# The second layer's attention weights turned in 32x32 blocks by the vector engine, and multiplied as 32-row matmuls on four row groups

## The chip, the core and the metric

The kernel runs on one core of a Trainium2 chip. The metric is the device time of one execution in microseconds; the median of three runs before the change is 858.31 us (855.99 to 860.19). The core has a matrix engine (TensorE, PE in the profile, its weight loads PEld), a vector engine (DVE), a scalar engine (ACT), a general engine (POOL) and a queue engine that issues most DMAs (SP). Each of them works through its own instructions in a fixed order, and they wait for one another by semaphores.

## The reference

Two layers over 512 latent and 256 context tokens of width 1024. Layer 0 is differential attention, layer 1, which the change is about, is grouped-query attention: 8 query heads of 128 share 2 K/V heads, and the 512 latent queries read all 768 keys. Cut to what matters:

```python
def sweep_attention(q, k, v):            # per block of 128 queries
    s = einsum('bqhgd,bkhd->bhgqk', q, k) * Dh ** -0.5
    p = softmax(s, axis=-1)
    return einsum('bhgqk,bkhd->bqhgd', p, v)

def gqa_mixer(h, hc, w_in, w_out, qk_g, cos, sin):
    q, k, v, z = split(h @ w_in)         # k and v from latent and context tokens
    q = rope(rms_norm(q, qk_g[0])); k = rope(rms_norm(k, qk_g[1]))
    return (sweep_attention(q, k, v) * silu(z)) @ w_out

x = x + gate * rms_norm(gqa_mixer(...), post_g)
```

## The kernel before

Every product of the layers is done as three matmuls of operands that are split into a rounded high part and the remaining low part (`mm3`: high x high, high x low, low x high; L145 to L147). The high part is made by a copy on ACT, the low part by a subtraction on DVE or POOL.

Layer 1 goes in these steps. First K and V are projected for six blocks of 128 tokens. V stays in SBUF as a high and a low part, `vh` and `vl`, tokens on the partitions (L1315, L1316). Then Q is projected in four pairs of heads (`q_proj`, on which a rope on DVE and POOL follows) and the gate path Z in eight heads (`z1_proj`). These two are fill work: generators of single matmuls, listed in `FILL1`, which a planner puts between the steps of attention. Their weights come as 512 KB loads on SP into two buffers (`raw`), are split by ACT (L199) and by POOL or DVE (L200), and are held in a few slots.

Attention is a set of streams of steps with due times, in `flow`. A clock in the planner counts matmul time; the step that is due first is written next, and as long as none is due, fill work is written. The streams are `S_` (scores), `T_` (transposes), `M_` (multiplication with V), `X_` (`q_tr`, which transposes Q of a head) and `Y_` (ten steps that sum the rows of the output gate from 512 KB loads, on DVE). The final order on each engine is then set by a scheduler that has the priorities of these steps.

One score unit is one head and 128 queries: six matmuls of 384 columns into one of two PSUM buffers of two banks (`sc`), the maximum on DVE (L1398), its scaling (L1401), the exponential with its sum on ACT (L1404), the reciprocal on DVE (L1405) and the normalisation on POOL (L207) into an SBUF tile `p`, queries on the partitions. The keys have to be on the partitions for the product with V. So for each head, each half of 256 queries and each pair of 128-key blocks, TensorE transposes four 128x128 blocks into a PSUM bank (L1419), ACT copies the high part out (`ah`, L1422), DVE subtracts the low part (`al`, L1423), and six matmuls with 128 rows and 256 columns add the product to the result of this half (`pv_mm`, L152). There are 48 such chunks: 8 heads, 2 halves, 3 pairs of blocks. ACT moves the result to SBUF (L1436), POOL multiplies it with the gate (L1366). At the end `tail1` splits the gated heads (L1482, L1483), the first quarter of the output projection starts with the heads that are there (`out_head`), and the other columns, the sums of squares, the residual `x1` (in SBUF since layer 0) and the stores follow.

## Time and profile before

| what | value |
|---|---|
| median of three runs | 858.31 us |
| profiled execution, its time | 855.26 us |
| profiled execution, its span | 853.5 us |
| mean granted TensorE clock | 0.985 |
| HBM read and written | 70.56 MB, 2.10 MB |

All durations below are those of the profiled execution; its own time is 1.8 us above its span. A row of a group of instructions reads: line, engine, operation, output and inputs, shapes, count, then the busy time in us and the mean of one in ns, then the engine's idle time before them and what ended it. A row of the timeline reads: start and length in us, engine, line, operation, count, and in brackets the idle time before it. For TensorE the length of a matmul contains the passage through the array, so matmuls overlap in the rows, and the distance between starts tells what one costs.

### The profile page before, as it was taken

The page shows a single profiled execution, that of the slowest core. Times are in us where ns is not written, and L with a number is a line of the kernel's source. Part 1 is how long each engine was busy: PE and PEld are TensorE (multiplying, and loading weights), DVE is VectorE, ACT ScalarE, POOL GpSimd, SP SyncE. Part 2 cuts the span into 40 slices and gives each one's busy share as a digit, 9 for nine tenths or more (in the row PEclk, how much of TensorE's full clock was granted, in tenths as well). Part 3 has the DMA queues.
Part 4 walks back from the last instruction along what each step waited for, and adds up shares of the span by engine and source line. Part 5 has one row for each costly group of instructions (what it writes and reads, how often), then busy time and mean ns, then how long its engine had stood idle before and what let it go on. Part 6 is the DMA issues. An engine that isn't in the chain of part 4 may idle for free. (4 is left out here: it accounts for less than half of the span.)

```text
span 853.5 us, 14255 instructions
## 1 busy us (share of the span) xinstructions
PE 808.6 (95%) x5472; PEld 710.3 (83%) x5472; DVE 498.5 (58%) x897; ACT 455.0 (53%) x1001; POOL 412.4 (48%) x390
## 2 busy tenths in 40 slices
PE   7899998999999999999899999989999989999997
PEld 5578887789786899698798898779999879999986
DVE  4425556763666755674437963477346576665634
ACT  5324456565465544565436953465445556676731
POOL 4333564746356663365631321465578736544201
PEclk8999999999999999999899999999999999999999
DMA  9933210122123241222320106030223232210112
GB/s 302 347 100 124 87 38 26 68 80 78 35 95 128 93 143 63 90 72 87 136 95 29 48 27 220 4 105 26 99 99 100 75 99 76 75 50 26 51 48 99
DMA packets 41540, 77.77 MB, mean 91 GB/s; under 512 B 3584, under 2 KB 18688, under 8 KB 41472
## 3 DMA queue, kind: packets, MB, share of 16 engines
q1 hardware_dynamic: 38048, 71.71, 25.4%
q10 hardware_dynamic: 3424, 5.15, 1.7%
q8 instruction: 43, 0.70, 0.3%
q14 instruction: 25, 0.20, 0.1%
HBM read 70.56 MB, written 2.10 MB: 85 GB/s over the span
## 5 line engine op out<-in xcount | busy, mean ns | idle before, releaser
L145 PE MATMUL bk<-whi,h 128*128 128x256 f32 (+1 forms) x592 | 177.3, 302 | 5.1 <-DVE u L1184 3.6
L146 PE MATMUL bk<-wlo,h 128*128 128x256 f32 (+1 forms) x592 | 176.7, 299 | 0.7 <-DVE wlo L200 0.7
L147 PE MATMUL bk<-whi,h 128*128 128x256 f32 (+1 forms) x592 | 176.1, 300 | 0.7 <-DVE h L1222 0.6
L145 PE MATMUL bk<-h,whi 128*128 128x512 f32 (+2 forms) x416 | 148.0, 356 | 2.5 <-DVE vlo L798 1.3
L146 PE MATMUL bk<-h,whi 128*128 128x512 f32 (+2 forms) x416 | 146.3, 352 | 0.0
L147 PE MATMUL bk<-h,wlo 128*128 128x512 f32 (+2 forms) x416 | 146.0, 352 | 0.0
L200 POOL TENSOR_TENSOR wlo<-raw,whi 128x1024 fp32r<-128x1024 f32 x46 | 114.0, 2483 | 61.6 <-ACT whi L199 61.4
L145 PEld LDWEIGHTS bk<-whi,h 128*128 128x128 f32 x592 | 112.7, 190 | 13.8 <-DVE u L1184 3.2
L207 POOL TENSOR_SCALAR p<-p,sm 128x768 f32<-128x768 f32 (+1 forms) x80 | 70.1, 878 | 105.9 <-DVE sm L872 54.0
L146 PEld LDWEIGHTS bk<-wlo,h 128*128 128x128 f32 x592 | 112.8, 190 | 5.7 <-issue 1.3
L147 PEld LDWEIGHTS bk<-whi,h 128*128 128x128 f32 x592 | 112.5, 191 | 4.8 <-DVE h L1222 1.1
L145 PEld LDWEIGHTS bk<-h,whi 128*128 128x128 f32 x416 | 79.3, 191 | 13.9 <-issue 1.8
L869 ACT ACTIVATE p<-sc,sm 128x768 f32<-128x768 f32 (+1 forms) x68 | 59.6, 878 | 54.0 <-DVE sm L866 49.1
L147 PEld LDWEIGHTS bk<-h,wlo 128*128 128x128 f32 x416 | 79.2, 191 | 10.0 <-issue 2.6
L146 PEld LDWEIGHTS bk<-h,whi 128*128 128x128 f32 x416 | 79.4, 191 | 7.7 <-issue 1.3
L199 ACT CAST whi<-raw 128x1024 fp32r<-128x1024 f32 x64 | 67.2, 1051 | 31.2 <-PE bk L146 11.7
L866 DVE TENSOR_REDUCE sm<-sc 128x1 f32<-128x768 f32 (+1 forms) x68 | 60.6, 917 | 17.6 <-PE sc L861 17.6
L929 ACT CAST ah<-bk 128x512 fp32r<-128x512 f32 x56 | 32.0, 589 | 36.7 <-PE bk L926 21.8
L877 DVE SCALAR_TENSOR_TENSOR p<-p,sm,p 128x768 f32<-128x768 f32 (+1 forms) x34 | 43.3, 1274 | 11.1 <-POOL p L207 8.7
L753 POOL TENSOR_TENSOR qr<-qr,rope 128x512 f32<-128x512 f32 x14 | 23.7, 1690 | 50.8 <-DMA sw<-qr 36.8
L861 PE MATMUL sc<-qk,qk 64*128 64x384 f32 (+1 forms) x396 | 44.7, 353 | 2.2 <-ACT p L900 1.2
L930 DVE TENSOR_TENSOR al<-bk,ah 128x512 fp32r<-128x512 f32 x56 | 37.5, 684 | 13.6 <-ACT ah L929 13.5
(247 smaller groups left out, 1721.1 us busy)
## 6 DMA issues: line engine op xcount, KB each, us to landing
raw<-in_a_w SPq DMA_DIRECT2D x30, 512.0 KB, 3.5
araw<-in_ada_w SPq DMA_DIRECT2D x12, 1024.0 KB, 5.1
raw<-in_b_w SPq DMA_DIRECT2D x20, 512.0 KB, 3.5
ag<-in_ada_w SPq DMA_DIRECT2D x32, 256.0 KB, 6.4
raw<-in_w_out SPq DMA_DIRECT2D x16, 512.0 KB, 3.5
sw<-qr ACTq DMA_DIRECT2D x32, 128.0 KB, 2.9
raw<-in_ada_w SPq DMA_DIRECT2D x8, 512.0 KB, 3.7
xt<-in_x SPq DMA_DIRECT2D x4, 512.0 KB, 5.4
```

The source lines that it names most:

```text
L145: nc.tensor.matmul(o, ahi, bhi, start=start, stop=False)
L146: nc.tensor.matmul(o, ahi, blo, start=False, stop=False)
L147: nc.tensor.matmul(o, alo, bhi, start=False, stop=stop)
L199: nc.scalar.copy(hi, r)
L200: eng.tensor_tensor(lo, r, f32(hi), ALU.subtract)
L207: (nc.vector if eng == "v" else nc.gpsimd).tensor_scalar(dst, src, s_, 1.0, ALU.mult, ALU.mult)
L861: prev = nc.tensor.matmul(sc[m][:, j if nk == T else m, :w], a[r, tok], b[r, c], start=i == 0, stop=i == 2)
L866: nc.vector.tensor_reduce(mx, scv, AX.XY if nk == T else AX.X, ALU.max, negate=True)
L869: nc.scalar.activation(pv_, scv, AF.Exp, bias=mx, accum_out=l[:, m:m + 1])
L877: nc.vector.scalar_tensor_tensor(ps_[0], pt, r, ps_[0], ALU.mult, ALU.add)
L929: nc.scalar.copy(ah, tr)
L930: nc.vector.tensor_tensor(al, tr, f32(ah), ALU.subtract)
```

## The change

The probabilities are no longer transposed by TensorE. `p_turn` turns each 128x768 tile `p` on DVE, in 32x32 blocks: partition 32i + r of the result holds key 32k + r, for all 24 blocks k of 32 keys, of the 32 queries 32i to 32i + 31. So each group of 32 partitions has all keys, but only its own queries. Eight turns (two heads, four blocks of queries) fill one tile `pT`, of which there is one.

`pv1_burst` then multiplies two heads at once. For each of 24 blocks of keys and each of the three high and low terms it issues four matmuls with 32 rows and 256 columns, one for each group of 32 partitions, into four PSUM banks; in bursts 0 to 2 two of the banks are one of the score buffers. There are four bursts (numbered 0 to 3 below) of 288 such matmuls, in place of 288 matmuls with 128 rows. High parts are still made on ACT, low parts by DVE and POOL in turn (`ECL`), in chunks of two blocks of keys, with four buffers for each part. V has to lie on every group of 32 partitions: it is stored to DRAM, high and low parts together (`v_dram`), and loaded four times over for each of the two K/V heads (`v_load4`), 3.1 MB each, the second time after burst 1, into the same tile.

Around this: the streams are now `S_`, `B_` (bursts and `tail1`) and `R_` (turns); a unit's due time goes by `TSU` and a burst's 8.6; the list of fill work is in another order; the gate's steps come at every third unit; the last pair of heads, not only the last half of a head, is gated and split after the last burst (`last_pair`), with `out_head` over six heads, and a part of the next output columns is written ahead (`o_next`). To make room, `x1` is stored to DRAM and loaded again at the end, and layer 1's context columns lie in tiles of their own (`h1c`).

```diff
-FILL1 = (('z', 0), ('q', 2), ('q', 1), ('z', 2), ('z', 1), ('q', 3), ('z', 3), ('z', 4), ('z', 5), ('z', 7), ('z', 6))
+FILL1 = (('q', 1), ('z', 0), ('z', 1), ('z', 2), ('q', 2), ('z', 3), ('z', 4), ('q', 3), ('z', 5), ('z', 6), ('z', 7))
...
-GSTEP = 2
+GSTEP = 3
...
+KB = 24
+ECL = 'vp'
+PB = 5
+TSU = 3.4
+LR = 4.5
+LB = 3.5
...
+    x1 = [bp.tile([P, D], F32, name=f"x1_{t}", bufs=1) for t in range(NQ)]
+    h1c_hi, h1c_lo = [bp.tile([P, KT, C], F32R, tag="h1c", name=nm("h1c"), bufs=2) for _ in range(2)]
+    x1_dram = dram.tile([S, D], F32, name="x1_dram")
+    v_dram = dram.tile([T, 2, 2, P], F32, name="v_dram")
...
+        if m < NQ:
+            nc.sync.dma_start(x1_dram[m * P:(m + 1) * P, :], xd)
...
-                    nc.scalar.copy(vh[:, m, :], o)
-                    nc.vector.tensor_tensor(vl[:, m, :], o, f32(vh[:, m, :]), ALU.subtract)
+                    if m // 2 not in vsp:
+                        vsp[m // 2] = t1p.tile([P, 2, 512], F32R, tag="gp", name=nm("vs"), bufs=4)
+                    vs = vsp[m // 2][:, m % 2].rearrange("p (g h d) -> p g h d", g=2, h=2)
+                    og = o.rearrange("p (g d) -> p g d", g=2)
+                    nc.scalar.copy(vs[:, :, 0], og)
+                    nc.vector.tensor_tensor(vs[:, :, 1], og, f32(vs[:, :, 0]), ALU.subtract)
                     close(o)
+                    nc.sync.dma_start(v_dram[m * P:(m + 1) * P], f32(vs))
...
+        vrep = {}
+
+        def v_load4(g):
+            vrep[g] = t1p.tile([P, KB, 2, P], F32R, tag="vr", name=nm("vr"), bufs=1)
+            for i in range(4):
+                nc.sync.dma_start(
+                    f32(vrep[g][32 * i:32 * i + 32]), v_dram[:, g].rearrange("(k p) h d -> p k h d", p=32))
+
+        v_load4(0)
...
-        def s1_units(h, ms):
...
+        pts, pTs = {}, {}
+
+        def s1_unit(h, m):
+            g = h // 4
+            qa, qb = qT[h]
+            sl = slice(m * P, (m + 1) * P)
+            sc = sc2()
...
+            pts[h, m] = pt
+
+        def p_turn(h, m):
+            b, u = h // 2, h % 2 * NQ + m
+            if u == 0:
+                pTs[b] = t1q.tile([P, KB, 256], F32, tag="pT", name=nm("pT"), bufs=1)
+            nc.vector.transpose(
+                pTs[b][:, :, u * 32:u * 32 + 32], pts.pop((h, m)).rearrange("p (k n) -> p k n", n=32))
+
+        def pv1_burst(b):
+            need = 3 if b < 3 else 4
+            while len(lru) < need:
+                ok_ = piece()
+                assert ok_ or len(lru) >= need
+            g, pT = b // 2, pTs.pop(b)
+            os, prev = [pj(256) for _ in range(4 if b == 3 else 2)], None
+            if b < 3:
                 sc = sc2()
...
+                os += [sc[:, 0, :256], sc[:, 1, :256]]
+            for c in range(KB // 2):
+                ah = t1q.tile([P, 512], F32R, tag="ah", name=nm("ah"), bufs=4)
+                al = t1q.tile([P, 512], F32R, tag="al", name=nm("al"), bufs=4)
+                src = pT[:, 2 * c:2 * c + 2].rearrange("p k n -> p (k n)")
+                nc.scalar.copy(ah, src)
+                VP[ECL[c % 2]].tensor_tensor(al, src, f32(ah), ALU.subtract)
                 for e in range(2):
...
+                    kb = 2 * c + e
+                    for t, (v, a) in enumerate(((0, ah), (1, ah), (0, al))):
+                        for i in (3, 2, 1, 0):
+                            r = slice(32 * i, 32 * i + 32)
+                            with after(prev):
+                                prev = nc.tensor.matmul(
+                                    os[i], vrep[g][r, kb, v, :], a[r, e * 256:e * 256 + 256],
+                                    start=kb == 0 and t == 0, stop=kb == KB - 1 and t == 2)
+            gp = t1p.tile([P, 2, 512], F32, tag="gp", name=nm("gp"), bufs=4)
+            pairs[b] = gp.rearrange("p h (m i n) -> p i h m n", m=NQ, i=4)
+            for j in range(2):
+                gT1[2 * b + j] = gp[:, j, :]
+            for i, o in enumerate(os):
+                ov_ = o.rearrange("p (h m n) -> p h m n", h=2, m=NQ)
+                (nc.scalar.copy if i % 2 else nc.vector.tensor_copy)(pairs[b][:, i], ov_)
+                if i < 2 or b == 3:
                     close(o)
...
+            for h in (2 * b, 2 * b + 1):
+                done1.add(h)
+                gate_mul1(h)
+            if b == 1:
+                v_load4(1)
...
-        def last_half(j):
...
+        def last_pair():
+            for h in (KT - 2, KT - 1):
+                VP[EGL].tensor_tensor(gT1[h], gT1[h], szt1[h], ALU.mult)
+            split_g1((KT - 2, KT - 1))
...
-            split_g1(range(KT - 1))
-            last_half(0)
+            split_g1(range(KT - 2))
             w_o.append(get_wout(1, *OUTC1[0]))
             o_pre.extend(sc_quarter(OUTC1[0][1]))
-            add(out_head(o_pre, ghi, glo, w_o[0], OUTC1[0][1]))
+            add(out_head(o_pre, ghi, glo, w_o[0], OUTC1[0][1], KT - 2))
...
-            for ch in range(2):
...
+            for m in range(NQ):
+                n = len(S_)
+                st_ = Step(lambda h=h, m=m: s1_unit(h, m), 1.05, [(qtr[h], 2.5)], at=at_ + TSU * n + 8.6 * ((n + 5) // 8 - 1 if n > 3 else 0))
+                if n >= 2:
+                    st_.lag.append((S_[-2], SLAG1))
+                if n >= PB:
+                    st_.lag.append((R_[n - PB], 0.0))
+                S_.append(st_)
+                R_.append(Step(lambda h=h, m=m: p_turn(h, m), 0.0, [(st_, LR)]))
+                if B_:
+                    R_[-1].lag.append((B_[-1], 0.0))
+            if h == KT - 1:
+                B_.append(Step(tail1, 0.0, [(S_[-1], 0.0)]))
+            if j:
+                B_.append(Step(lambda p=p: pv1_burst(p), 8.6, [(R_[-1], LB)]))
...
-        flow(1, [S_, T_, M_, X_, Y_])
+        flow(1, [S_, B_, R_, X_, Y_])
         drain()
         w_o = w_o[0]
+        last_pair()
+        x1_ = t1q.tile([P, KB, 256], F32, tag="pT", name=nm("x1"), bufs=1)
+        x1 = [x1_[:, 4 * m:4 * m + 4].rearrange("p k n -> p (k n)") for m in range(NQ)]
+        for m in range(NQ):
+            nc.sync.dma_start(x1[m], x1_dram[m * P:(m + 1) * P, :])
+        c, n = OUTC1[1]
+        o_next, w_next = pj(n), {k: ws.get(k) for k in wout_keys(1, c, n) if ws.has(k)}
+        kn = 1024 // n * len(w_next)
+        run(out_proj(o_next, ghi, glo, list(w_next.values()), 0, n, 0, kn))
...
+                elif qi == 1 and m == 0:
+                    o = o_next
+                    run(out_proj(o, ghi, glo, w, m, n, kn))
```

Three places in the programs, by their order on an engine.

On PE in the middle of layer 1's attention, before: `sc` are score buffers, `bk` banks, `kh`, `kl`, `qh`, `ql` the parts of K and Q, `p` the probabilities, `vh` and `vl` V.

```order
L147 MATMUL sc_73<-kh,ql_7956 128x384
L152 MATMUL bk_70<-ah_7983,vh 128x256 x2
L152 MATMUL bk_70<-ah_7983,vl 128x256 x2
L1419 MATMUL bk_71<-ident,p_7810 128x128
L1419 MATMUL bk_71<-ident,p_7864 128x128
L1419 MATMUL bk_71<-ident,p_7810 128x128
L1419 MATMUL bk_71<-ident,p_7864 128x128
L152 MATMUL bk_70<-al_7984,vh 128x256 x2
L152 MATMUL bk_70<-ah_8009,vh 128x256 x2
```

On PE at the start of burst 0, now: the end of the unit ahead of it (two units, 12 matmuls, stand between the last unit that the burst needs and the burst), the first matmuls of the burst, and then projection; `whi`, `wlo` and `h` are a Q projection, `vr` the copied V.

```order
L152 MATMUL sc_74<-kh,qh_6869 128x384
L153 MATMUL sc_74<-kl,qh_6869 128x384
L154 MATMUL sc_74<-kh,ql_6870 128x384
L1466 MATMUL sc_75<-ah_7086,vr_6347 128x256 x2
L1466 MATMUL bk_71<-ah_7086,vr_6347 128x256
L1466 MATMUL bk_72<-ah_7086,vr_6347 128x256
L1466 MATMUL sc_75<-ah_7086,vr_6347 128x256 x2
L1466 MATMUL bk_71<-ah_7086,vr_6347 128x256
L1466 MATMUL bk_72<-ah_7086,vr_6347 128x256
L152 MATMUL bk_70<-whi_6735,h_689_5197 128x256
L153 MATMUL bk_70<-wlo_6736,h_689_5197 128x256
L154 MATMUL bk_70<-whi_6735,h_690_5198 128x256
```

The transposes (L1419) between the multiplications are gone, and a burst stands in one piece, without other matmuls in it; only burst 0 has 14 projection matmuls after its eighth, of which the first three are shown. Bursts 1 and 2 stand behind projection matmuls, 2.9 and 5.6 us of them at the distances of the profile.

On PE at the last score units, before (`h` and `whi` are a Z projection, as fill work):

```order
L147 MATMUL bk_68<-h_689_5199,wlo_7913 128x512
L145 MATMUL sc_72<-kh,qh_8159 128x384
L146 MATMUL sc_72<-kl,qh_8159 128x384
L147 MATMUL sc_72<-kh,ql_8160 128x384
L145 MATMUL sc_72<-kh,qh_8159 128x384
L146 MATMUL sc_72<-kl,qh_8159 128x384
L152 MATMUL bk_71<-ah_8340,vh 128x256 x2
L152 MATMUL bk_71<-ah_8340,vl 128x256 x2
L1419 MATMUL bk_69<-ident,p_8263 128x128
L1419 MATMUL bk_69<-ident,p_8308 128x128
```

On PE behind burst 2, now (`ac` and `ones_r` are the column sum of the gate):

```order
L1466 MATMUL bk_72<-al_8828,vr_8140 128x256
L152 MATMUL sc_74<-kh,qh_8400 128x384
L153 MATMUL sc_74<-kl,qh_8400 128x384
L154 MATMUL sc_74<-kh,ql_8401 128x384
L152 MATMUL sc_74<-kh,qh_8400 128x384
L153 MATMUL sc_74<-kl,qh_8400 128x384
L154 MATMUL sc_74<-kh,ql_8401 128x384
L374 MATMUL bk_72<-ac_8950,ones_r 128x512
L152 MATMUL sc_75<-kh,qh_8400 128x384
L153 MATMUL sc_75<-kl,qh_8400 128x384
L154 MATMUL sc_75<-kh,ql_8401 128x384
```

Six units, one behind the other, stand behind burst 2 with nothing but that column sum between them; the fill work has been used up before, and the first quarter of the output projection comes after the sixth.

On DVE in burst 2, now (`h` are the split heads, L1519 the low part of them, L207 a weight's low part, L1459 a low part of the attention, L1429 and L1433 the small steps of a unit):

```order
L1459 TENSOR_TENSOR al_8520<-pT_8160,ah_8519 128x512
L1429 TENSOR_TENSOR sm_8499<-sm_8497,qrs_8240 128x1
L1459 TENSOR_TENSOR al_8576<-pT_8160,ah_8575 128x512
L1433 RECIPROCAL sm_8454<-sm_8454 128x1
L1433 RECIPROCAL sm_8502<-sm_8502 128x1
L1519 TENSOR_TENSOR h_1276_9031<-gp_7422,h_1275_9030 128x512 x2
L1519 TENSOR_TENSOR h_1276_9031<-gp_8133,h_1275_9030 128x512 x2
L207 TENSOR_TENSOR wlo_8971<-raw_8968,whi_8970 128x1024
L1459 TENSOR_TENSOR al_8632<-pT_8160,ah_8631 128x512
L1459 TENSOR_TENSOR al_8688<-pT_8160,ah_8687 128x512
L1459 TENSOR_TENSOR al_8744<-pT_8160,ah_8743 128x512
L1459 TENSOR_TENSOR al_8800<-pT_8160,ah_8799 128x512
```

On DVE at the end of the attention before, the splits stand in the same way between low parts:

```order
L1423 TENSOR_TENSOR al_8535<-bk_68,ah_8534 128x512
L200 TENSOR_TENSOR wlo_8587<-raw_8584,whi_8586 128x1024
L1483 TENSOR_TENSOR h_1288_8601<-g_974_6952,h_1287_8600 128x512
L1483 TENSOR_TENSOR h_1288_8601<-g_1029_7222,h_1287_8600 128x512
L1483 TENSOR_TENSOR h_1288_8601<-g_1069_7440,h_1287_8600 128x512
L1483 TENSOR_TENSOR h_1288_8601<-g_1121_7706,h_1287_8600 128x512
L1483 TENSOR_TENSOR h_1288_8601<-g_1176_7977,h_1287_8600 128x512
L1483 TENSOR_TENSOR h_1288_8601<-g_1212_8181,h_1287_8600 128x512
L1423 TENSOR_TENSOR al_8555<-bk_69,ah_8554 128x512
L1423 TENSOR_TENSOR al_8624<-bk_68,ah_8623 128x512
```

In both, splits and a weight's low part stand between two low parts of the attention; what has moved is that four splits now come between the low parts of burst 2, where six heads were split at once before. Behind these rows DVE has two turns (L1441) of the last pair and the evictions of the burst (L1475).

144 lines of the change are left out of this document (49 added, 95 removed).

## The prediction

> **What bounds the kernel now.** I read the page's first part, then the busy time by stretches, then PE's waits in the stage that is changed.
>
> ```profile
> span 853.5 us, 14255 instructions
> PE 808.6 (95%) x5472; PEld 710.3 (83%) x5472; DVE 498.5 (58%) x897; ACT 455.0 (53%) x1001; POOL 412.4 (48%) x390
> ```
>
> ```profile
> 675.00:695.00 20.00, 18.53 (x114) 15.66 (x113) 14.92 (x26) 10.36 (x21) 8.89 (x9) 1.00 0.40 118
> 695.00:715.00 20.00, 17.73 (x132) 17.02 (x132) 13.77 (x23) 12.25 (x24) 10.48 (x9) 1.00 0.34 106
> 612.00:848.00 236.00, 231.05 (x1568) 214.64 (x1566) 140.03 (x282) 132.34 (x296) 116.79 (x125) 1.00 0.22 72
> ```
>
> After the stretch come its length and the busy times of PE, PEld, DVE, ACT and POOL, then the granted clock, the DMA share and GB/s. Layer 1's Q and Z projections, attention and output lie between 612 and 848 us. PE is idle there for 236.00 - 231.05 = 4.95 us, most of it in two 20 us stretches, while DVE works 59% of the time, ACT 56% and POOL 49%. So TensorE's order is the clock of this stage: a matmul that leaves it is worth its time, and a wait that is put into it costs its time.
>
> ```profile
> PE bk L1355 <- DVE al L1423: 2.3, 1, 2.3
> PE bk L1355 <- DVE ql L1359: 0.7, 1, 0.7
> ```
>
> These are PE's longest waits after 613 us (total, times, longest): it is DVE, late in its own queue, that holds PE.
>
> **The change part by part.** *Transposes on PE go.* A matmul's own time is longer than its share of the pipeline, so I take distances between starts.
>
> ```profile
> 805.38 0.28 PE L146 MATMUL sc<-wlo,h 128*128 128x256 f32 x1
> 805.50 0.60 PE L1419 MATMUL bk<-ident,p 128*128 128x128 f32 x4
> 805.86 0.48 PE L152 MATMUL bk<-al,vh 128*128 128x256 f32 x2
> 806.18 0.28 PE L147 MATMUL sc<-whi,h 128*128 128x256 f32 x1
> L1419 PE MATMUL bk<-ident,p 128*128 128x128 f32 x192 | 29.0, 274 | 0.2 <-ACT g L1436 0.2
> ```
>
> A 256-column matmul moves the next one by 0.12 us (805.38 to 805.50). Four transposes and two such matmuls take 806.18 - 805.50 = 0.68 us, so four transposes cost 0.68 - 0.24 = 0.44. There are 192/4 = 48 such sets: **-21.1 us**.
>
> *The multiplication itself.* Before, 16 chunks of 3 x 6 = 288 matmuls of 256 columns, 288 x 0.12 = 34.6 us. Now 4 bursts of 24 x 3 = 72 groups, and each group is four 32-row matmuls of 256 columns on four row groups. If the four run side by side, this is again 288 x 0.12. No 32-row matmul is in the trace, but layer 0's scores are pairs of 64-row ones:
>
> ```profile
> 122.02 0.75 PE L890 MATMUL sc<-qk,qk 64*128 64x256 f32 x10
> 382.07 1.00 PEld L861 LDWEIGHTS sc<-qk,qk 64*128 64x128 f32 x12 [0.17 <-issue]
> ```
>
> Five pairs of 256 columns, of which the last matmul takes 0.28: (0.75 - 0.28)/4 = 0.1175 us a pair, what a single full matmul takes. Two row groups run fully side by side, and their weight loads do too: twelve loads in 1.00 us are 0.083 each. I take 0.1175 for four as well: **0**. The bounds are this and 2 x 0.1175 = 0.235, where only two run at once; 0.1175 is the nearer row, since nothing in the pairs shows a limit.
>
> *Change of row groups.* Going into 32-row work and out of it is seen once in the trace for 64 rows:
>
> ```profile
> 381.54 0.60 PE L926 MATMUL bk<-ident,p 128*128 128x128 f32 x4
> 382.07 1.32 PE L861 MATMUL sc<-qk,qk 64*128 64x384 f32 x12
> 383.32 0.38 PE L152 MATMUL bk<-al,vhi 128*128 128x256 f32 x1
> 383.54 0.35 PE L147 MATMUL bk<-h,wlo 128*128 128x384 f32 x1
> ...
> 634.24 0.34 PE L145 MATMUL sc<-kh,qh 128*128 128x384 f32 x1
> 634.42 0.33 PE L146 MATMUL sc<-kl,qh 128*128 128x384 f32 x1
> 634.59 0.34 PE L145 MATMUL sc<-kh,qh 128*128 128x384 f32 x1
> ```
>
> 384 columns take 0.175 (634.24 to 634.59 for two). The transposes should let the pairs start at 381.98, and they start at 382.07; six pairs should take 1.05 and take 1.25; the next matmul takes 0.22 for 0.12. Together 0.09 + 0.20 + 0.10 = 0.4 us. There are five entries (the first burst is split in two by 14 projection matmuls): **+2.0 us**.
>
> *New waits of PE.* The durations:
>
> ```profile
> L1398 DVE TENSOR_REDUCE sm<-sc 128x1 f32<-128x768 f32 x32 | 30.4, 949 | 4.7 <-PE sc L147 4.6
> L1401 DVE TENSOR_TENSOR sm<-sm,qrs 128x1 f32<-128x1 f32 x32 | 7.0, 218 | 0.2
> L1405 DVE RECIPROCAL sm<-sm 128x1 f32<-128x1 f32 x32 | 5.1, 158 | 14.3 <-ACT p L1404 14.1
> L1423 DVE TENSOR_TENSOR al<-bk,ah 128x512 fp32r<-128x512 f32 x48 | 32.3, 685 | 22.3 <-ACT ah L1422 22.3
> L200 DVE TENSOR_TENSOR wlo<-raw,whi 128x1024 fp32r<-128x1024 f32 x8 | 9.8, 1227 | 4.6 <-ACT whi L199 4.4
> L1404 ACT ACTIVATE p<-sc,sm,qrs 128x768 f32<-128x768 f32 x32 | 31.9, 998 | 20.2 <-DVE sm L1401 13.4 <-PE bk L1419 4.3 <-DVE qrs L1340 2.3
> L1404 ACT ACTIVATION_READ_ACCUMULATOR p<-sc,sm,qrs 128x1 f32 x32 | 6.4, 200 | 0.0
> L1422 ACT CAST ah<-bk 128x512 fp32r<-128x512 f32 x48 | 27.3, 589 | 15.7 <-PE bk L1419 14.4 <-PE bk L152 0.7
> L207 POOL TENSOR_SCALAR p<-p,sm 128x768 f32<-128x768 f32 x64 | 62.6, 978 | 88.8 <-DVE sm L872 44.6 <-DVE sm L1405 36.5 <-DVE sm L1401 3.9
> L366 POOL TENSOR_TENSOR ac<-gate,ac 128x512 fp32r<-128x512 f32 x2 | 2.6, 1294 | 0.0
> L877 DVE SCALAR_TENSOR_TENSOR p<-p,sm,p 128x768 f32<-128x768 f32 (+1 forms) x34 | 43.3, 1274 | 11.1 <-POOL p L207 8.7
> L1457 DVE TENSOR_SCALAR gate<-raw,scol x2: 486/845/1204, 631.7 to 686.5; 128x512 f32<-128x512 f32 x2
> ```
>
> The trace has no DVE transpose. The nearest rows are DVE's other full passes over 768 elements: between L1423 (512 in 0.685) and L200 (1024 in 1.227) lies 0.95, the reduce at 0.949 says the same. Ends: 0.73 (L1457's shortest, 0.486 for 512, times 1.5) and 1.27 (L877). I take 0.95; 32 turns put 30.4 us on DVE, and 24 low parts that go to POOL take 24 x 0.685 = 16.4 off it and put 24 x 1.294 = 31.1 on POOL. DVE then works 154 us of the stage and POOL 148, of some 225: neither is the bound on average, so the cost lies where the order lets a burst wait.
>
> - Burst 0. Its last unit is followed on PE only by two further units, 12 x 0.175 = 2.1 us. The chain from that unit to the first high part is 0.949 + 0.218 + 0.998 + 0.200 + 0.158 + 0.978 + 0.95 + 0.589 = 5.0. The rest is 2.9, with an estimate of 0.4 for hand-overs: **+3.3** (2.9 to 7, the upper end if DVE is also late with its queue).
> - After burst 2 the fill work is used up, and six score units stand on PE back to back. A unit holds one of two PSUM buffers for 6 x 0.175 + 0.949 + 0.218 + 0.998 = 3.2, with hand-overs 3.5; the sixth ends 2 x 3.5 + 2 x 1.05 = 9.1 us after the first starts, where PE has 6.3 us of work. Meanwhile DVE has 8 turns, 6 reduces with their two small ones, and seven instructions of up to 512 columns: 7.6 + 8.0 + 4.8 = 20.4 as an upper end, less 0.08 for each of 33 (the rows below), less the two turns that still fall into the burst: 15.9. PE has 9.1 + 0.5 + 72 x 0.12 = 18.2 until burst 3. **+3.5** (2.8 to 8).
>
> ```profile
> 767.54 0.68 DVE L1423 TENSOR_TENSOR al<-bk,ah 128x512 fp32r<-128x512 f32 x1
> 768.14 0.95 DVE L1398 TENSOR_REDUCE sm<-sc 128x1 f32<-128x768 f32 x1
> ```
>
>   Back to back, DVE starts the next instruction 0.60 after one that lasts 0.68.
> - Within burst 2, DVE has four splits and a weight split between its second and third low part: 4 x 0.685 + 1.227 = 4.0 us, against four chunks in the buffers, 4 x 6 x 0.1175 = 2.8: **+1.0** (0 to 3). POOL's six low parts, 7.8 us, fit into a burst's 72 x 0.1175 = 8.5.
> - Starts of bursts 1 and 2, which 2.9 and 5.6 us of projection cover: **+2.0** (0 to 5). After burst 3 the first of 32 wide matmuls waits for a PSUM bank: **+0.7**; the eviction, the gate product and the split of the last pair hide behind those.
>
> *DMA.* V goes out in six stores and comes back four times over, 4 x 0.79 = 3.1 MB for each K/V head; the first need is some 60 us away, the second 27 us behind burst 1.
>
> ```profile
> GB/s 302 347 100 124 87 38 26 68 80 78 35 95 128 93 143 63 90 72 87 136 95 29 48 27 220 4 105 26 99 99 100 75 99 76 75 50 26 51 48 99
> raw<-in_w_out SPq DMA_DIRECT2D x16, 512.0 KB, 3.5
> ```
>
> At 347 GB/s that is 9 us, at 512 KB in 3.5 us 21: hidden, **0**. Behind the second copy on SP wait two gate loads and the output weights, needed over 15 us later. If that cover went, DVE would wait in its queue for the gate rows, up to some 6 us. The residual's reload has over 20 us of output matmuls before it.
>
> *Old idle time.* The 4.95 us came from DVE's queue. I let half go: **-2.4**, between -4.9 and 0.
>
> Sum: -21.1 + 2.0 + 3.3 + 3.5 + 1.0 + 2.0 + 0.7 - 2.4 = **-11.0 us**. The profiled execution took 855.26 (span 853.5), so it would take 844.3. The median of the three runs is 858.31, 3.05 above that one, so the median would be **847.3**.
>
> **Rivals.**
> - *Four row groups give less than fourfold.* If a group takes a third of the way from 0.1175 to 0.235, 0.157, a burst grows by 72 x 0.039 = 2.8 us and four by 11.3: 858.6, no gain. For it: nothing in the trace runs four at once. Against it: two cost nothing. The Trainium skill, "TensorE: Matmul & The Clock Gate", Part 3 under "Measured speedup vs the span model", gives 3.07x for four row tiles of 512 columns; that would be 0.12 x 4/3.07 = 0.156 a group (an estimate from that page) and the same end. Chance 0.12.
> - *TensorE's supply of instructions becomes the bound, and it is slower.* A group needs eight instructions in 0.1175 us, 0.015 each, for 8.5 us on end. The densest row, the pairs, has four in 0.1175, 0.029 each. If that is the limit, a group takes 0.235, a burst 16.9 and four 33.8 us more; longer bursts hide some 4 us of the waits: 847.3 + 33.8 - 4 = 877. From 0.157 a group on the gain is gone. For it: no row shows a higher rate for as long. Against it: the pairs run at the pace of their columns and show no limit. The same page, Part 1, "Wait — 56ns, not 53.3ns?", has 62 ns for each matmul with one way of decoding, 0.248 a group, an estimate that ends near the same; no run here shows it. Chance 0.12.
> - *DVE becomes the bound.* If a turn takes two passes, 1.9 us, DVE gets 30 us more. Between bursts 2 and 3 it would need 15.9 + 7.6 = 23.5 for PE's 18.2, +5.3; each other burst, by an estimate, some 2.5: 860. For it: no row has the instruction. Against: all full passes take one. Chance 0.10.
>
> **How the numbers follow.** The forecast, 838 to 854, has 0.60. Better than 838, with waits at their lower ends (-21.1 + 2.0 + 2.9 + 2.8 + 0.7 - 4.9 = -17.6, 840.7, and a little below if turns are short), has 0.04, and slower by other mishaps 0.02. The range 837 to 866 leaves out the second rival and little else. A measurement tells about 0.5% from no change, 4.3 us: faster than 854.0 are the forecast, the better case and a sixth of the first rival, 0.66; between 854.0 and 862.6 most of the first and third rivals, 0.18; slower the rest, 0.16.
>
> **What would show it.** Right: the groups of the new line start 0.12 us apart with four starts within some 0.02; PE idle rises before burst 0 and among the six units after burst 2, and by no more than some 10 us; the turn is near 0.95; PE's busy time falls by about 20. Wrong: group starts 0.16 or more apart, a turn near 1.9, or PE waiting for the copied V.

## The result and the profile after

The changed kernel takes 890.85 us (median of 4 runs, 888.05 to 891.76), the kernel before on the same chip 858.57 us: a ratio of **1.037** (95% interval 1.034 to 1.041). It is 32 us slower; faster by 1.3% was forecast. Measured once more on another chip the ratio was 1.0415 (1.038 to 1.045); experiments below are set against 1.039, the middle of the two, or against the second where they ran beside it. Up to 612 us the two profiles do the same work, the changed one some 2 us of matmuls behind, so nearly all of it lies in layer 1's attention and output. The profiled execution has a span of 889.3 us (before 853.5).

The top of the page of the changed kernel (busy time, share, instructions), and the granted TensorE clock in 40 slices:

```profile
span 889.3 us, 15670 instructions
PE 812.6 (91%) x6144; PEld 706.8 (79%) x6144; DVE 537.0 (60%) x912; ACT 455.6 (51%) x992; POOL 450.3 (51%) x413
PEclk9799999999999999998999999999997998977899
```

PE is busy for longer (812.6 us for 808.6) although 192 transposes are gone, and the clock falls in the last quarter of the program. The longest waits of PE behind 612 us (total, times, longest) were 2.3, 0.8 and 0.7 us before. Now:

```profile
PE sc L152 <- ACT p L1432: 9.1, 6, 3.5
PE sc L152 <- ACT qh L1387: 7.5, 2, 4.0
PE sc L1466 <- ACT p L1432: 4.9, 1, 4.9
PE sc L1466 <- ACT ah L1458: 3.1, 2, 2.6
PE bk L1384 <- DVE tb L1273: 3.1, 1, 3.1
PE bk L375 <- POOL ac L373: 2.8, 1, 2.8
PE sc L1466 <- DVE al L1459: 2.2, 1, 2.2
```

The busy times by stretch, bursts and what lies between them in turn (length, busy PE, PEld, DVE, ACT, POOL, granted clock, DMA):

```profile
639.40:687.60 48.20, 38.85 (x219) 35.19 (x219) 38.61 (x67) 27.76 (x60) 33.20 (x29) 0.91 0.36 109
687.60:701.30 13.70, 13.67 (x303) 12.51 (x303) 8.45 (x10) 7.44 (x13) 11.93 (x9) 0.83 0.02 4
701.30:739.60 38.30, 31.25 (x192) 28.41 (x188) 29.77 (x55) 21.73 (x47) 27.71 (x25) 0.96 0.28 88
739.60:751.60 12.00, 11.77 (x289) 10.71 (x289) 9.26 (x9) 6.36 (x11) 9.86 (x7) 0.84 0.09 30
751.60:795.50 43.90, 36.15 (x176) 30.95 (x176) 31.98 (x63) 24.32 (x56) 25.56 (x26) 0.84 0.65 144
795.50:809.00 13.50, 10.73 (x290) 10.19 (x290) 9.78 (x10) 7.66 (x14) 6.94 (x6) 0.87 0.13 41
809.00:836.50 27.50, 21.82 (x113) 19.11 (x113) 20.82 (x36) 14.22 (x26) 13.87 (x12) 0.75 0.06 20
836.50:846.10 9.60, 9.54 (x289) 8.77 (x288) 7.14 (x5) 4.97 (x8) 7.28 (x5) 1.00 0.19 58
```

A burst of 72 groups at 0.1175 us is 8.5 us; the four take 13.7 (with 14 projection matmuls among them), 12.0, 13.5 and 9.6. Between bursts DVE is busy for 73 to 80% of the time, where it had 59% before.

**An account of the 36 us.** I gave each matmul the distance to the next start that its form has at full clock (0.118 us for 256 columns, 0.1745 for 384, 0.233 for 512, 0.109 for a transpose, 0.0294 for a 32-row one) and summed them; the rest is either a wait (from the end of one matmul to the start of the next) or matmuls that follow each other more slowly.

| from 612 us to the end of the output matmuls | before | after | difference |
|---|---|---|---|
| matmuls at full clock | 227.1 | 208.0 | -19.1 |
| waits of PE | 4.7 | 36.8 | +32.2 |
| matmuls slower than at full clock | 3.6 | 25.9 | +22.2 |
| sum | 235.4 | 270.7 | +35.3 |

So the change saves what it was to save: 19.1 us here, and 17 matmuls (2.0 us) that stood ahead of 612 us before now stand behind it. It loses 54 us elsewhere. The last line is mostly the clock: 18.6 of the 25.9 us lie in stretches at half clock, 7.3 outside them, where the kernel before has 3.6. Slices of 1 us around the start of burst 1 (length, busy PE with its matmuls, granted clock, DMA), and PE's groups there (start, length):

```profile
735.00:736.00 1.00, 0.00 (x0) 1.00 0.36 61
736.00:737.00 1.00, 0.00 (x0) 0.84 0.94 385
737.00:738.00 1.00, 0.00 (x0) 0.50 0.20 78
...
742.00:743.00 1.00, 1.00 (x26) 0.50 0.00 0
743.00:744.00 1.00, 1.00 (x32) 0.74 0.00 0
744.00:745.00 1.00, 1.00 (x36) 1.00 0.00 0
```

```profile
739.62 0.58 PE L1466 MATMUL sc<-ah,vr 32*128 32x256 f32 x2 [4.94 <-ACT p L1432]
...
742.14 0.41 PE L1466 MATMUL sc<-al,vr 32*128 32x256 f32 x2
742.15 0.41 PE L1466 MATMUL bk<-al,vr 32*128 32x256 f32 x2
742.35 0.41 PE L1466 MATMUL sc<-ah,vr 32*128 32x256 f32 x2
...
743.59 0.28 PE L1466 MATMUL sc<-ah,vr 32*128 32x256 f32 x2
743.71 0.28 PE L1466 MATMUL sc<-ah,vr 32*128 32x256 f32 x2
```

Two rows are one group of four: it starts 0.01 us apart, so all four row groups run side by side. Groups follow one another by 0.21 us at half clock (742.14 to 742.35) and by 0.117 at full clock (743.59 to 743.71). PE waited 4.9 us, the clock was halved from 736.7 on, and stayed so for 6.8 us; the first 17 groups were paid nearly double. The windows at half clock behind 612 us add up to 51 us (671.8 to 678.7 is the first, 815.2 to 828.9 the last).

What burst 1 waited for stands in DVE's and ACT's rows:

```profile
733.29 1.53 DVE L1497 SCALAR_TENSOR_TENSOR gate<-raw,scol,gate 128x512 f32<-128x512 f32 x1 [1.37 <-DMA raw<-in_ada_w]
734.75 0.94 DVE L1426 TENSOR_REDUCE sm<-sc 128x1 f32<-128x768 f32 x1
735.61 0.67 DVE L1388 TENSOR_TENSOR ql<-bk,qh 128x512 fp32r<-128x512 f32 x1
736.21 1.51 DVE L1497 SCALAR_TENSOR_TENSOR gate<-raw,scol,gate 128x512 f32<-128x512 f32 x1
737.65 0.68 DVE L1459 TENSOR_TENSOR al<-pT,ah 128x512 fp32r<-128x512 f32 x1
738.25 0.15 DVE L1429 TENSOR_TENSOR sm<-sm,qrs 128x1 f32<-128x1 f32 x1
738.49 0.99 ACT L1432 ACTIVATE p<-sc,sm,qrs 128x768 f32<-128x768 f32 x1 [3.10 <-DVE sm L1429]
```

The burst needs a score buffer. That buffer is free after the exponential (L1432), which needs the small step L1429. That step stands in DVE's queue behind two gate sums, of which the first waited for its 512 KB load, and behind a reduce and two low parts. From 731.92, where the wait for the load begins, to 738.25 are 6.3 us; the wait and the two sums are 4.4 of them. Turns, V and the first low parts were there.

### The profile page after: what moved, and what is told of

The parts are those of the page before. It is cut to its first block, busy times and chain, and to the rows that moved or that the text cites. A ratio compares the mean times of both kernels' runs of the same rounds, so it can differ in the third digit from the quotient of the medians.

```text
span 889.3 us, 15670 instructions
## 1 busy us (share of the span) xinstructions
PE 812.6 (91%) x6144; PEld 706.8 (79%) x6144; DVE 537.0 (60%) x912; ACT 455.6 (51%) x992; POOL 450.3 (51%) x413
## 5 line engine op out<-in xcount | busy, mean ns | idle before, releaser
L152 PE MATMUL bk<-whi,h 128*128 128x256 f32 (+1 forms) x560 | 169.8, 306 | 5.6 <-DVE u L1199 3.6
L153 PE MATMUL bk<-wlo,h 128*128 128x256 f32 (+1 forms) x560 | 169.6, 304 | 0.8 <-DVE wlo L207 0.8
L154 PE MATMUL bk<-whi,h 128*128 128x256 f32 (+1 forms) x560 | 168.2, 303 | 0.0
L207 POOL TENSOR_TENSOR wlo<-raw,whi 128x1024 fp32r<-128x1024 f32 x46 | 115.1, 2506 | 65.1 <-ACT whi L206 63.8
L152 PEld LDWEIGHTS bk<-whi,h 128*128 128x128 f32 x560 | 108.7, 194 | 14.8 <-DVE u L1199 3.2
L153 PEld LDWEIGHTS bk<-wlo,h 128*128 128x128 f32 x560 | 108.8, 194 | 6.2 <-issue 1.7
L154 PEld LDWEIGHTS bk<-whi,h 128*128 128x128 f32 x560 | 108.0, 194 | 3.8
L936 ACT CAST ah<-bk 128x512 fp32r<-128x512 f32 x56 | 32.0, 588 | 35.7 <-PE bk L933 19.6
L1432 ACT ACTIVATE p<-sc,sm,qrs 128x768 f32<-128x768 f32 x32 | 31.8, 992 | 33.8 <-DVE sm L1429 29.4
```

The source lines that it names most:

```text
L152: nc.tensor.matmul(o, ahi, bhi, start=start, stop=False)
L153: nc.tensor.matmul(o, ahi, blo, start=False, stop=False)
L154: nc.tensor.matmul(o, alo, bhi, start=False, stop=stop)
L207: eng.tensor_tensor(lo, r, f32(hi), ALU.subtract)
L936: nc.scalar.copy(ah, tr)
L1432: nc.scalar.activation(pt.rearrange("p (j n) -> p j n", j=2), scv, AF.Exp, scale=sr, bias=nmx, accum_out=l)
```

## The experiments

Ratios are to the kernel before, measured beside each run.

**Low parts on one engine (low_on_dve).**

```diff
-ECL = 'vp'
+ECL = 'vv'
```

> All low parts of the bursts on DVE, none on POOL; TensorE's order is unchanged. In the changed kernel a low part takes 0.68 us on DVE and 1.28 on POOL when alone, and 1.75 on both when they run at the same time. Theory A (the two engines hold one another up, both operands lying in SBUF): no low part above 0.75 us, a burst's chunk no longer waits after every second group of twelve, bursts 1 to 3 shorter by 1 to 2 us each, the time 4 to 8 us below the changed kernel's 890.9, near 884. Theory B (DVE is the bound by the amount of its work): DVE gets 24 more low parts, 24 x 0.68 = 16 us, and the time rises by 3 to 8 us.

Measured: 1.034 (1.031 to 1.037), -4 us against 1.039, about the difference of the two measurements of the changed kernel. The mechanism is plain in the rows. In the changed kernel, burst 1 (timeline, eight low parts on two engines), and below it seven low parts in burst 1 of this run, on DVE alone:

```profile
743.35 6.30 DVE L1459 TENSOR_TENSOR al<-pT,ah 128x512 fp32r<-128x512 f32 x4 [0.34 <-ACT ah L1458]
743.97 6.83 POOL L1459 TENSOR_TENSOR al<-pT,ah 128x512 fp32r<-128x512 f32 x4
```

```profile
740.74 4.81 DVE L1459 TENSOR_TENSOR al<-pT,ah 128x512 fp32r<-128x512 f32 x7 [0.34 <-ACT ah L1458]
```

Two engines needed 750.80 - 743.35 = 7.45 us for eight (0.93 each), one needs 0.69 each. Both operands now lie in SBUF (before, one lay in PSUM). Alone, a low part takes 0.68 us on DVE and some 1.27 on POOL; a pair of them takes 7.45/4 = 1.86 here, nearly the 1.95 of one after the other. The Trainium skill, "SBUF — State Buffer", "SBUF: two separate sides", has a lock that a DVE operation with two SBUF inputs and a GpSimd operation take in turn; the rows agree. The four bursts went from 48.8 to 44.1 us in all, burst 3 to the 8.8 us of its matmuls. Theory A holds for the low parts and the bursts; the gain of the whole is at its lower end and not clear of the noise.

**V's copies (one_v_copy, v_long_rows).**

```diff
-                                    os[i], vrep[g][r, kb, v, :], a[r, e * 256:e * 256 + 256],
+                                    os[i], vrep[0][r, kb, v, :], a[r, e * 256:e * 256 + 256],
...
-            if b == 1:
-                v_load4(1)
```

```diff
-    v_dram = dram.tile([T, 2, 2, P], F32, name="v_dram")
+    v_dram = dram.tile([2, 32, KB, 2, P], F32, name="v_dram")
...
-                    f32(vrep[g][32 * i:32 * i + 32]), v_dram[:, g].rearrange("(k p) h d -> p k h d", p=32))
+                    f32(vrep[g][32 * i:32 * i + 32]), v_dram[g])
```

> The second fourfold load of V is left out (heads 4 to 7 are multiplied with the first K/V head's V); everything else is as in the changed kernel. Theory A (the copy, 17 us at 188 GB/s, holds up the gate rows and the output weights behind it on the queue, DVE and ACT wait for these, and with them TensorE): the three waits of TensorE at 775 to 785 us, 3.1 + 4.0 + 0.6 us, and the half clock from 777.7 to 791.3 go, the time falls by 8 to 12 us to about 881. Theory B (these waits come from DVE's amount of work): the waits stay, the time moves by less than 2 us.

> V lies in DRAM so that each partition loads 24 KB in one piece in place of 24 pieces of 1 KB; bytes are the same (the stores of V are four in place of one per block). Theory A (the size of the pieces sets the rate): each fourfold load takes about 9 us in place of 17, at some 350 GB/s, the waits at 636 and at 775 to 785 us shrink by half or more, the time falls by 4 to 10 us. Theory B (16 engines are full whatever the pieces): the load stays at 17 us and the time within 2 us.

Measured: 1.037 (1.034 to 1.040) without the second copy, 1.042 (1.039 to 1.046) with long pieces: no change that can be told. Long pieces leave the loads as they are (the last piece lands 19.3 us after its issue, 18.9 in the changed kernel), as theory B had it. Without the copy DVE's wait on the gate's load at 772 us is gone, but the 4.0 us wait at 779 us is there again (3.9 us at 773 us): ACT is now late through another chain, DVE's sums and Z's steps. Theory A fails as to the time: what was the last of several late chains is not what the time hangs on. The first copy was not taken away.

**Idle matmuls behind burst 2 (idle_fill).**

```diff
+        def spare(n):
+            o = pj(256)
+            for _ in range(n):
+                nc.tensor.matmul(o, kh[:, 0, :P], kh[:, 0, :256], start=True, stop=True)
+                yield 256 / 2400.0
...
+
+        add(spare(60))
```

> 60 idle matmuls of 256 columns (7.0 us of TensorE's time, a result that nobody uses) are put as fill work between the six units behind burst 2, where TensorE waits 5.7 us in all and its clock is half from 815.2 to 828.9. Theory A (the waits bring the clock down, and the half clock is what makes this stretch long): the clock stays full there, a unit's six matmuls take 1.05 us in place of 1.9, and the time falls by 2 to 6 us although 7 us of work are added. Theory B (the waits alone cost): the idle matmuls fill waits of 5.7 us and add the rest, the time rises by 0 to 3 us.

Measured: 1.046 (1.041 to 1.050), some 6 us up, or 4 against the second measurement. The stretch between bursts 2 and 3 grew from 27.5 to 29.6 us in the profile and its clock from 0.75 to 0.88, but not to 1: the idle matmuls stood ahead of units that were ready (31 of them up to 818.0 us, where the next unit's buffer was free from 816.4 on). Theory A fails, since the time rose; the run doesn't separate clock and waits.

**The amount of DVE's work (half_turn, double_turn), beside the changed kernel again (after_again).**

```diff
-                pTs[b][:, :, u * 32:u * 32 + 32], pts.pop((h, m)).rearrange("p (k n) -> p k n", n=32))
+                pTs[b][:, :KB // 2, u * 32:u * 32 + 32], pts.pop((h, m))[:, :T // 2].rearrange("p (k n) -> p k n", n=32))
...
-                src = pT[:, 2 * c:2 * c + 2].rearrange("p k n -> p (k n)")
+                src = pT[:, 2 * c % 12:2 * c % 12 + 2].rearrange("p k n -> p (k n)")
```

```diff
+            for pt in (pts[h, m], pts.pop((h, m))):
+                nc.vector.transpose(pTs[b][:, :, u * 32:u * 32 + 32], pt.rearrange("p (k n) -> p k n", n=32))
```

> The changed kernel once more, unaltered, on the chip of the next three runs, so that they can be compared with it on one chip. Every theory: the ratio to the kernel before is 1.037 again, within 0.004.

> DVE turns only the first half of the keys (12 of 24 blocks of 32), and the burst reads that half twice; TensorE's number of matmuls is unchanged. Theory S (between two bursts DVE has more to do than TensorE, 121 us of busy time against 112 us of matmuls in the four stretches, and the bursts cover none of it): 32 x 0.49 = 16 us less on DVE, TensorE's waits fall by 8 to 16 us, with the half clock behind them the time falls by 10 to 20 us. Theory C (the waits come from the order of the fill work and from the half clock that every wait brings, DVE's load is not the limit): under 4 us.

> Every tile is turned twice on DVE into the same place, 32 x 0.97 = 31 us more on DVE; nothing else changes. Theory S (DVE is the longer engine between bursts): the time rises by 20 to 35 us. Theory C (order and clock): DVE is busy 60% of the time, most of the second turns fit into its idle time, and the time rises by less than 10 us.

Measured: 1.0415 for the changed kernel, 1.035 (1.031 to 1.040) with half turns (-5 us for 16 us less on DVE, not clear of the noise), 1.063 (1.059 to 1.067) with double ones (+18 us for 31 us more, part of which is the second turn in the chain ahead of each burst). The waits are 38 us with half turns, but that profile is of the slowest of the four executions, 891.4 us, which is no faster than the changed kernel. The amount of DVE's work is a part of the loss, not all of it: theory S overstates the first, theory C understates the second.

**Score units inside the bursts (units_in_bursts).** Besides a burst in three steps, the edit that counts is the priority of bursts below that of units, low parts on DVE, other due times for units, and one score buffer left to the units:

```diff
-HOT1 = (1100, 2900, 2600, 2600, 2100)
+HOT1 = (1400, 900, 2600, 2600, 2100)
...
-                B_.append(Step(lambda p=p: pv1_burst(p), 8.6, [(R_[-1], LB)]))
+                for k in range(3):
+                    B_.append(Step(lambda p=p, k=k: pv1_part(p, k), 8.6 / 3, [(R_[-1], LB)] if k == 0 else [(B_[-1], 1.0)]))
```

> Bursts 0 to 2 are no longer in one piece: a burst is planned in three parts with a lower priority than the score units, so that four units of the next pair stand inside each burst, some 30 matmuls apart, and only two units are left behind burst 2; low parts are all on DVE. Theory S: the units' work on DVE, ACT and POOL now lies beside the bursts, the waits between bursts shrink, and the time falls by 10 to 20 us against the changed kernel, less 12 further changes of row groups at up to 0.4 us, 5 us. Theory C: as long as the fill list is the same the waits stay, and the time moves by less than 4 us beyond those 5. Theory D (many changes between 128-row and 32-row work are costly): the time rises.

Measured: 1.060 (1.056 to 1.064), 16 us slower than the changed kernel. Theory D forecast a rise, but for changes of row groups; the reason is in PE's waits:

```profile
PE sc L154 <- ACT p L1434: 17.0, 14, 3.5
PE bk L1386 <- POOL q L1278: 7.8, 3, 5.4
```

A burst keeps one of the two score buffers, so units inside it follow each other by the whole chain of one buffer, and PE waits for that fourteen times. The try says nothing on interleaving with more buffers.

**The gate sums (no_gate, no_gate_vv_half, gate_own_buffer_vv, gate_in_kv_vv).**

```diff
         def gate1_part(half, k2):
+            if k2:
+                return
             acc = gate1[:, half * 512:half * 512 + 512]
```

> Of the eight 512 KB loads of gate rows and their sixteen sums on DVE only the two first loads with four sums are left (the output gate is that of two of eight blocks of rows); everything else is as in the changed kernel. Theory G (DVE's queue holds a gate sum that waits for its load, and the small steps of the score units stand behind it; the chain back from burst 1's wait has 17.5 us of such loads in 25): the waits of TensorE at 669, 728, 735 and 775 to 785 us shrink, the time falls by 8 to 16 us against the changed kernel (ratio 1.022 to 1.031 to the kernel before). Theory S (DVE's amount of work between bursts): 12 sums x 0.98 = 12 us less on DVE, as with half of the turns (16 us less gave 5 us), 3 to 5 us.

> Three omissions and changes at once: gate sums as in the run before, low parts all on DVE, and only half of the keys turned. If waits on DVE's queue make up the loss (theories G and S together), 28 us less work, no load waited for there and no holding up by POOL: the waits after 612 us fall from 37 to under 20 us, the half clock from 55 us to under 25, and the time by 20 us or more, to a ratio of 1.015 or below. If the order in which matmuls are written on TensorE itself is the cause (theory O), the waits stay above 30 us and the time falls by under 10 us.

```diff
-            gw = wp.tile([P, 1024], F32, tag="raw", name=nm("raw"), bufs=2)
+            gw = t1q.tile([P, 1024], F32, tag="graw", name=nm("graw"), bufs=1)
```

> Gate rows are loaded into a buffer of their own, no longer into the two that the weights use, so that a load can start as soon as the sum before it is done; high and low parts of the bursts have three buffers in place of four to make room, low parts are all on DVE. Correct result. Theory G: gate sums no longer wait for their loads, and weight loads no longer for gate sums; the time falls by 6 to 14 us. Theories S and O: as with low parts on DVE alone, 2 to 7 us.

```diff
+        gparts = [(half, k2) for half in range(2) for k2 in range(4)]
-        for what, m in KV:
+        for kvi, (what, m) in enumerate(KV):
+            if kvi >= 8 and gparts and (kvi - 8) % 1 == 0:
+                gate1_part(*gparts.pop(0))
```

> All eight gate loads and sixteen sums are moved ahead of attention, between the projections of K and V (540 to 612 us, where DVE is busy some 55%), and all low parts are on DVE; correct result. Theory G: 8 to 14 us below the changed kernel, a ratio of 1.022 to 1.031, still slower than the kernel before, since the waits at the starts and in the bursts and behind burst 2 stay. Theory S (only the amount of DVE's work counts): the same amount in all, at most 3 us from low parts on DVE.

Measured: 1.0255 (1.023 to 1.028) without most of the sums, -11 us; with low parts on DVE and half turns besides 1.024 (1.021 to 1.026), -13; with a buffer of their own (low parts on DVE, and three buffers in place of four for high and low parts) 1.039 (1.037 to 1.042), nothing; and with all sums moved ahead of attention and low parts on DVE **1.023** (1.019 to 1.026), -14 us. The amount of work alone is not it: 12 us less of sums gave 11 us, 16 us less of turns 5. DVE's waits on the gate's loads behind 612 us, in the kernel before, the changed one and the one with a buffer of their own:

```profile
DVE gate L1459 <- DMA raw<-in_ada_w: 5.4, 5, 2.1
DVE gate L1497 <- DMA raw<-in_ada_w: 6.2, 3, 4.0
DVE gate L1497 <- DMA graw<-in_ada_w: 19.6, 5, 10.4
```

With the first sums (3.4 and 2.3 us) these are 8.8 us before and 8.5 in the changed kernel: DVE is held up alike, and only the changed kernel pays for it. The buffer of its own made these waits longer, so that run does not show what the kernel would do without them. What fits all rows is that sums, and their waits for loads, stand between the score units' small steps in DVE's queue; how much the waits and how much the sums cost was not separated. In the last run the wait for the score buffer at burst 1 is gone (PE's waits):

```profile
PE sc L152 <- ACT qh L1405: 10.2, 3, 5.5
PE sc L152 <- ACT p L1450: 7.1, 5, 3.0
PE sc L1484 <- ACT ah L1476: 3.8, 3, 2.0
PE bk L375 <- POOL ac L373: 2.8, 1, 2.8
```

PE still waits 26.5 us and runs 20 us of slow matmuls there, and between 500 and 612 us, where the sums now are, it gets through 6.5 us less of matmuls (93.3 us in place of 99.8). It is the best version with the change, and slower than the kernel before. With three causes taken away at once (no_gate_vv_half) 26.4 us of waits are left, at the start, at the bursts and at the six units, between the under 20 of theories G and S together and the over 30 of theory O.

**The clock at one burst (burst1_warm).**

```diff
+                for _ in range(36 if b == 1 and c == 0 else 0):
+                    with after(prev):
+                        prev = nc.tensor.matmul(os[0], vrep[g][:, 0, 0, :], ah[:, :256], start=True, stop=True)
```

> 36 idle matmuls of 256 columns (4.2 us) stand ahead of burst 1, on the first high part, into a bank that the burst then overwrites; in the changed kernel TensorE waits 4.9 us there and the clock is half from 736.7 to 743.5 us. Theory of the clock (a wait of some 2 us or more within a window of 3.41 us halves the clock of the next windows): no half clock around burst 1, its groups start 0.117 us apart from the first on, the burst takes 10.3 in place of 12.0 us, the time falls by 1 to 2 us. If the clock does not follow the waits: the groups of the burst's first part still take 0.213, and the time rises or stays.

Measured: no half clock from 736.6 to 780.9 us, and the first 23 groups of burst 1 follow one another by 0.117 us, from the second on. So the half clock there is the wait's doing. The burst took 11.6 us, since it now ran into its low parts (waits of 0.4, 0.9 and 0.3 us), and the whole kernel 1.050 (1.046 to 1.054): 4 us of idle matmuls and a later order elsewhere cost more than the 0.4 us that the burst gained. The clock is as forecast, the time is not.

**The same doubts put to the kernel before (before_no_gate, before_plus_turn, before_short_waits, before_long_waits).** The first has the edit of no_gate. The second and the last two:

```diff
+                for j in range(2):
+                    tt = t1q.tile([P, 12, 32], F32, tag="tt", name=nm("tt"), bufs=1)
+                    nc.vector.transpose(tt, pt[:, j * 384:j * 384 + 384].rearrange("p (k n) -> p k n", n=32))
```

```diff
+                        if (m, kt) in WAITS:
+                            with after(chain[0]):
+                                chain[0] = nc.tensor.matmul(wps, ones_r, ones_r, start=True, stop=True)
+                            nc.scalar.copy(wd, wps)
+                            for _ in range(NCP):
+                                nc.scalar.copy(wd4, f32(wd).unsqueeze(1).to_broadcast([P, 2, P]))
+                            with after(chain[0]):
+                                chain[0] = nc.tensor.matmul(wps, ones_r, wd4[:, 0], start=True, stop=True)
```

> The kernel before, with the gate sums cut as in the run no_gate (two of eight blocks of rows). TensorE's waits on DVE after 612 us are 4.7 us there in all. Theory G with the changed order (only where bursts stand in one piece does a late DVE stop TensorE): the time falls by 1 to 4 us, so that most of the 11 us in the changed kernel belong to the change. If the gate sums cost both kernels alike: 8 to 12 us.

> The kernel before, in which DVE also turns every tile of probabilities in 32x32 blocks into a scratch tile that nobody reads (two halves of 384, 0.97 us together, 31 us in all); transposes and multiplications stay as they are. Theory S (DVE's amount of work): DVE is busy 59% of the stage and would be at 72%, the time rises by 10 us or more. Theory O (the bursts in one piece expose each chain; interleaved, DVE's idle time takes the work): the time rises by less than 5 us.

> The kernel before, with eight waits of TensorE in the 64 wide matmuls of the output projection (each time a small product goes through three ACT copies and back before the next matmul; some 1.3 us each, 10 us in all, one in each 2.8 us of matmuls). Theory of the clock (a window of 3.41 us has to be idle for some 2 us): no half clock there, the time rises by the waits alone, 9 to 12 us. If any wait brings the clock down: 9 to 12 us and some 7 more.

> The kernel before, with four long waits at the same place (each through twelve ACT copies, an estimate of 3.5 to 4.5 us each, 14 to 18 us in all). Theory of the clock: each brings one or two windows of half clock with it, the matmuls behind it take up to twice as long for some 3 us, and the time rises by the waits and 1.5 to 3.4 us more for each of the four, 20 to 30 us in all. If the half clock costs nothing by itself: by the waits alone, 14 to 18 us.

> The kernel with eight short waits once more, for a profile. Theory of two thresholds (half from about 1.75 us of waits in a window of 3.41 us, and half for as long as a window holds 0.75 us or more): the first wait, 2.6 us, turns the clock to half, the next ones, 1.28 us in every 3 to 6 us, keep it there for most of the stretch, 15 us or more of half clock, 5 us or more of slow matmuls. Theory of one threshold: one window of half clock behind the first wait, and none behind the others.

Measured: 1.003 (1.001 to 1.005) without gate sums, no gain at all where the changed kernel has 11 us. 1.005 (1.003 to 1.007) with the turns beside the transposes, +4 us; one row of the stage and the group of turns, against the row 612 to 848 us of the kernel before (DVE 140.03, PE 231.05):

```profile
612.00:848.00 236.00, 229.69 (x1550) 212.76 (x1549) 172.54 (x343) 131.00 (x293) 114.88 (x124) 1.00 0.22 72
L1409 DVE STREAM_TRANSPOSE tt<-p 128x384 f32<-128x384 f32 x64 | 36.4, 569 | 4.8 <-POOL p L207 3.9
```

DVE is busy for 73% of the stage, as between the bursts, with 36 us of turns, and PE waits 6.3 us in place of 5. **Interleaved, the same DVE work is nearly free.** Theory O holds, S falls. Nobody reads these turns, so the run shows what DVE's time costs there, and not what a chain through a turn would cost.

The waits: 1.022 and, in the second run, 1.018 for the short ones, 1.036 (1.030 to 1.043) for the long ones. In both profiles the last of the added waits is covered by other matmuls, which leaves seven short and three long ones. From 812 us on, by the account above, the seven short ones are 10.5 us of waits and 4.9 of slow matmuls, and the run with long ones has 19.6 us of waits (16.9 in the three) and 9.5 of slow matmuls. Slices of the run with long waits, a wait at the end of the first, third and fifth row:

```profile
812.00:822.00 10.00, 6.18 (x43) 5.31 (x41) 4.44 (x9) 4.97 (x16) 0.00 (x0) 1.00 0.17 52
822.00:829.00 7.00, 3.37 (x9) 2.70 (x9) 0.00 (x0) 3.32 (x9) 0.00 (x0) 0.53 0.27 77
829.00:836.00 7.00, 4.24 (x19) 3.34 (x17) 0.69 (x1) 3.17 (x9) 0.42 (x2) 0.98 0.00 0
836.00:843.00 7.00, 4.55 (x11) 3.68 (x12) 0.00 (x0) 2.23 (x6) 0.00 (x0) 0.51 0.00 0
843.00:849.00 6.00, 3.45 (x16) 2.63 (x14) 0.69 (x1) 2.97 (x8) 0.40 (x2) 1.00 0.00 0
849.00:856.00 7.00, 4.35 (x11) 3.48 (x12) 0.00 (x0) 2.42 (x6) 0.00 (x0) 0.55 0.00 0
```

Each long wait brings 6.8 us of half clock, and costs half as much again as it lasts. Of the short ones the first, 2.8 us, did so once, where the first expectation had none; the other six, 1.28 us each, did not, and by then no window with waits fell into the half clock, so that it did not stay on as the second expectation had it.

## Why the prediction was wrong

The forecast was 847.3, with 837 to 866 as its range; the measured time is outside and on the other side.

- *Right.* The transposes' share; "the groups of the new line start 0.12 us apart with four starts within some 0.02"; the turn, 0.97 us for 0.95; the residual's reload. The two rivals on TensorE and the one of a turn in two passes are out: the supply of instructions reaches eight in 0.117 us, and four row groups take what one full matmul takes. The Trainium skill, "TensorE: Matmul & The Clock Gate", Part 3, "Measured speedup vs the span model", has 3.07-fold for four row tiles of 512 columns; this trace, with 256 columns, shows fourfold (0.117 us for four, 0.118 for one). That the second rival gave 877, the nearest to the result, is chance.
- *The step that failed* is "neither is the bound on average, so the cost lies where the order lets a burst wait". The prediction then looked at five places and gave them 10.5 us. PE waits 36.8 us, at nearly every point where it takes up work of DVE, ACT or POOL: 16.6 at the five places, and 20.1 at places that had no term (3.5 us at the first score unit, 6.7 at the units ahead of burst 0, 9.9 where Q's transposes and the units behind them wait for DVE, POOL or ACT). What the transposes and multiplications did before, besides their work, was to stand between score units all along: PE always had something to do that did not need the unit in hand. In one piece they cover only themselves. Two pairs of runs, with the same or nearly the same edit in both kernels, bear this out: leaving out gate sums gains 11 us in the changed kernel and none in the kernel before, and turns added on DVE cost 18 us and 4. That it is the one piece, and not the order of the fill work (`FILL1`, `GSTEP`), which changed with it, is argued: no run has one without the other.
- *Old idle time*, "I let half go: -2.4", had the wrong sign: PE's waits grew by 32 us. DVE's wait for gate rows stood in the prediction only as a risk of up to some 6 us; the gate sums cost 11 us as it is, shown by no_gate, and none in the kernel before, where without them PE still waits 4.6 us.
- *The clock* was in no term. Seven of the eight waits of 2 us or more drew the half clock or kept it on, 18.6 us in all in the account; the 3.5 us at 636 us drew none, as they fell half and half into two windows of the clock (see the last section). Not all of that is lost by itself, since slow matmuls partly stood where PE would have waited anyway, as burst1_warm shows; before_long_waits shows that it is a loss where matmuls are the bound. The trace of before had it: after 411 us the record of its clock has 6.8 us at half.
- *Low parts*, 24 x 0.685 on DVE and 24 x 1.294 on POOL, took 1.24 and 1.57. Price: 4.7 us of burst time between two profiles, and some 4 us of the whole, not clear of the noise.
- *Sizes.* Start of burst 0: 2.6 us of wait for 3.3, but 3.2 more at the units ahead of it. Six units: 5.7 for 3.5, but only 2.4 of it for a score buffer; 3.3 are the gate's column sum among them, which waits for DVE and POOL and had no term. Burst 2: 2.8 for 1.0. Starts of bursts 1 and 2: 4.9 for 2.0. After burst 3: 0.45 for 0.7. Change of row groups: the first group takes 0.22 us for 0.12, the last one 0.22 as well (751.31 to 751.53), and the first 384-column matmul behind it 0.28 (to 751.81) for 0.175, so some 0.3 each for 0.4. DMA: 3.5 us at 636 us for 0, where ACT stood 8.5 us behind a weight load that came after V's first copy; whether the copy is its cause was not tried.

What stays open: how the 26 us of waits divide that are left when gate sums, POOL's low parts and half of the turns are gone, what the other order of the fill work has cost, and whether units between smaller bursts with a third score buffer would bring the saving home.

## What to carry to other kernels

Before work is taken off the engine that sets the pace, ask what that work was covering: 21 us of transposes, spread between dependent steps, seem to have hidden more latency than they cost. Price a wait of TensorE at about one and a half times its length once 2 us of it can fall into one window of 3.41 us, and look through the in-order queue of the engine it waits for, for an instruction that stands on a DMA. Two engines that read SBUF with both operands may be slower together than one alone; measure the pair.
